# An encoder block in single-precision products: the residual added by accumulating transfers, and the work around the last weights laid out anew

## The chip, the core and the metric

The kernel runs on one core of one Trainium2 chip. The core has a matrix engine (TensorE, "PE" in the profile, with its weight loads as "PEld"), a vector engine (VectorE, "DVE"), an activation engine (ScalarE, "ACT"), a general engine (GpSimd, "POOL") that does no arithmetic here and only issues transfers, and a synchronisation engine (SyncE, "SP") that issues most transfers. 16 DMA engines move the bytes. The metric is device time in microseconds (us) from the first to the last instruction, lower is better; a kernel's time is the median of its runs.

## The reference

One layer of a bidirectional encoder on 512 tokens of width 2048, all in float32:

```python
h = rmsnorm(x, norm_attn)
proj = h @ w_in                                  # q, k, v of two groups of 8 heads
ya = dilated_attention(...); yb = diff_attention(...)
x = x + concat(ya, yb) @ w_out                   # called x1 below
h = rmsnorm(x, norm_ffn)
x = x + (silu(h @ w_gate) * (h @ w_up)) @ w_down # hidden width 5632
return rmsnorm(x, norm_final)
```

The change touches the two last lines alone. `rmsnorm(x, g)` is `x * r * g`, where `r` is one number for each token, the reciprocal root of the mean square. So the gate and up products can be taken of `x1 * g`, without `r`, and `r` can be multiplied in afterwards, token by token.

## The kernel before

**Products.** The matmuls take values of a rounded type (`F32R`). To keep float32's accuracy every operand is split into a high part and the rest: ACT rounds (`hi`), DVE subtracts (`lo = value - hi`), and `mm3` (lines 183 to 186) makes three matmuls of it. A split is therefore one ACT and one DVE instruction for each weight tile, at lines 120 and 121 for weights that go in as they are (`fetch`) and at lines 629 and 630 for weights that are first combined (`make`).

**Stages.** Queries, keys, values and both attentions come first; then the output projection (`unit_out`), which also stores `x1` to memory (`x1_kept`). Then come the gate and up products: 44 units of 128 hidden features each (`unit_gu`). They use a Strassen-like scheme with seven products instead of eight; `make` forms the sums of weights, `keep_combos` those of the activations, which go to memory (`combos`). The down product runs over most hidden features by the same scheme, in five chunks `c` of four or three pairs of feature tiles (`CHUNKS`), each in four units `u` of 512 output columns (`unit_dn`). What is left over goes in without the scheme: two feature tiles ahead of the chunks (`unit_first`) and four behind them (`unit_last`). `unit_last` runs over 4 token tiles `t` and 4 column groups `g`; each of the 16 groups is 12 matmuls of 512 columns, then `to_rest` and `finish`, which adds up the squares for the final norm and, at `g == 3`, scales the token tile and sends it out.

**The running sum.** `unit_first` copies its products to eight tiles `acc[u, l]` (`u` a column group, `l` a half of the tokens); half of each is stored negated, because `add` only adds. Every `unit_dn` adds its products to them. In the last chunk `add_x1` (lines 860 to 867) turns them into the residual sum: two instructions for each of 16 pieces compute `acc * r2 + x1`, with `r2` the token scale for one half and `nr2 = -r2` for the other, and `x1` loaded back by SP. `to_rest` adds the product of `unit_last`, again times `r2`. The scale `r` is thus multiplied in twice: in `unit_gu` into the gate and up values ahead of Silu (line 689, with the tile `rb2` that holds `r` along the tokens), where the up value `c11` and the other up values stay unscaled, and at the end for these.

**Order of the work.** PE's instructions run in the order in which the program lists them. Those of ACT, DVE, SP and POOL are put in order ahead of time by a planner, which simulates the program with a model of costs and takes the earliest listed instruction that is ready by this model; so a transfer or a split can stand well ahead of its place in the program, or behind it. Once planned, each engine runs its list strictly in order, waits included. Splits run three products ahead of PE (`product_of(..., ahead=3)`).

**Places.** Raw weights land in three staging tiles `st` (pool `wst`) or in `m0` to `m5`; split pairs lie in three rotating `hi`/`lo` pairs (`wsh`, `wsl`) and in `m6` to `m9`. The operands of the down product lie in seven large tiles (`cp0` to `cp5` and `w0`). The last eight weight pairs of `order` and the last four activation tiles (`act_tile`) take places that have become free by then: `late_tile` cuts them from `cp` tiles, three places from each; pairs 2, 3 and 4 use `wsh`/`wsl`. All of that is listed by `prepare_last` at one point, product 3 of the last unit (four `act_tile`, the gains of the final norm, two `fetch`), and by the first lines of `unit_last` (the other six `fetch`). Small constants lie in the pool `const`, which is placed first, so its size shifts the tiles behind it.

Of the kernel before, what the change touches and what calls it, by code (L numbers as in the profile page):

```python
# [45 lines left out]
def encoder_block(ctx: ExitStack, tc: tile.TileContext, io):  # L46
# [602 lines left out]
    def unit_gu(f):  # L649
# [23 lines left out]
        def after(i):  # L673
# [13 lines left out]
            elif i == 5:  # L687
                dve.tensor_add(g[:, first], gm[:, first], u2)
                dve.tensor_mul(g, g, pools["rb2"])
                act.activation(g, g, AF.Silu, scale=-1.0)  # L690
                dve.tensor_mul(out[0], c11, g[:, first])
# [48 lines left out]
    nr2 = const.tile([P, NT], F32, name="nr2")  # L740
# [27 lines left out]
    def unit_first():  # L768
# [3 lines left out]
        dve.tensor_scalar_mul(nr2, r2, -1.0)  # L772
        for u in range(DN):
# [11 lines left out]
            for t in range(NT):  # L785
                o = acc[u, t // 2][:, (t % 2) * 512:(t % 2 + 1) * 512]
                act.copy(o[:, :256], b[t][:, :256])
                act.activation(o[:, 256:], b[t][:, 256:], AF.Copy, scale=-1.0)

    def unit_dn(c, u):  # L790
# [17 lines left out]
        def add(h, l, x):  # L808
            dve.tensor_add(r[h, l], flat(x), r[h, l])
# [40 lines left out]
        for i in range(7):  # L850
            product(i, pairs[3:] if apart and i < 4 else pairs)
            after(i)
            if i0 == len(UNITS) - 1 and i == 3:
                prepare_last()
            yield
        if c == len(CHUNKS) - 1:
            for t in range(2):
                add_x1(t, u)

    def add_x1(t, u):  # L860
        x1 = w_tile()
        nc.sync.dma_start(x1, x1_kept[t, u])
        y = rest[t, u] = acc[u, t // 2][:, (t % 2) * 512:(t % 2 + 1) * 512]
        for h, r in enumerate((r2, nr2)):
            s = slice(h * 256, (h + 1) * 256)
            dve.scalar_tensor_tensor(y[:, s], y[:, s], r[:, t:t + 1], x1[:, s], op0=OP.mult, op1=OP.add)

    late = []

    def late_tile():  # L870

        n = len(late)
        if n % 3 == 0:
            late_tile.last = pools["xa"].tile([P, 7, 512], F32R, name=f"cp{(0, 1, 5, 2, 3)[n // 3]}")
        late.append(late_tile.last[:, 2 * (n % 3):2 * (n % 3) + 2].rearrange("p a q -> p (a q)"))
        return late[-1]

    def last_pair(i):
        if 2 <= i < 5:
            return wsh.tile([P, 1024], F32R, name="hi"), wsl.tile([P, 1024], F32R, name="lo")  # L880
        return late_tile(), late_tile()

    def prepare_last():
        for f in range(NF - CF, NF):
            act_tile(f, late_tile())
        load_gfin()
        fetch()
        fetch()
# [184 lines left out]
```

## Time and profile before

| | |
|---|---|
| median of 3 runs | 2227.66 us (2226.16 to 2230.18) |
| the profiled execution, its own time | 2229.82 us |
| its span, first to last instruction | 2228.0 us |
| granted TensorE clock, mean of the span | 0.992 |
| gate and up units | about 866 to 1748 us |
| `unit_first` and the five chunks | about 1748 to 2166.8 us |
| `unit_last` and the end | 2166.8 to 2228.0 us |

A window row of the profile gives a stretch, its length, the busy time of each engine with its number of instructions, then the granted clock (1.00 is full), the DMA engines' busy share and GB/s. A timeline row gives start, duration, engine, line, operation, output and inputs by the program's names, and in brackets the engine's idle time ahead of it and what ended it. A group row gives count, then total busy time and mean duration in ns, then idle time ahead of the group's instructions. Matmul durations overlap, since they are pipelined; the distance of their starts is their cost. Engine names with a "q" are the engine's instruction queue, which issues transfers.

### The profile page before, as it was taken

What the parts mean: (1) busy time and instruction counts of PE and PEld (TensorE: products, weight loads), DVE (VectorE), ACT (ScalarE), POOL (GpSimd) and SP (SyncE); (2) the same over time, 40 slices, a digit from 0 to 9 for tenths busy, and PEclk for the clock granted to TensorE, in tenths of its full rate; (3) what the DMA queues carried; (4) which work ended last, traced back from release to release, by engine and by line L of the source; (5) the groups of instructions that cost most, each with busy time, mean ns of one, the idle gap of its engine ahead of it and who ended that gap; (6) DMA issues with size and microseconds to landing.
All of it is one profiled execution on the core that took longest, in us unless ns stands there. A gap on an engine that the chain in (4) does not pass through costs nothing.

```text
span 2228.0 us, 37887 instructions
## 1 busy us (share of the span) xinstructions
PE 2195.6 (99%) x15754; PEld 2067.2 (93%) x15754; DVE 1663.9 (75%) x2373; ACT 999.4 (45%) x1486; POOL 10.4 (0%) x23
## 2 busy tenths in 40 slices
PE   9999999999999999999999999999999999999997
PEld 8888888888888888999999999999999899999995
DVE  5655555676787447888888888888887597888897
ACT  6333333545555344454444544445444443343443
POOL 0000000000000000000000000000000000000000
PEclk9999999999999999999999999999999999999999
DMA  8222222222222552354454444544445736446344
GB/s 301 84 78 76 85 77 76 76 76 68 67 76 91 165 180 85 124 169 147 132 169 147 165 147 134 170 147 159 151 132 164 312 114 245 156 166 236 114 138 138
DMA packets 86908, 308.59 MB, mean 139 GB/s; under 512 B 10032, under 2 KB 11952, under 8 KB 84304
## 3 DMA queue, kind: packets, MB, share of 16 engines
q1 hardware_dynamic: 81696, 267.11, 36.4%
q0 software_dynamic: 2736, 34.87, 3.8%
q10 hardware_dynamic: 2304, 4.20, 0.5%
q8 instruction: 123, 2.02, 0.4%
q14 instruction: 49, 0.40, 0.1%
HBM read 261.31 MB, written 44.83 MB: 137 GB/s over the span
## 4 chain that ended last, share of the span: by engine, by line
PE 92%; DVE 4%; DMA 2%; ACT 1%; issue 1%; SPq 0%; ACTq 0%; DVEq 0%
PE bank L184 30%; PE bank L186 29%; PE bank L185 29%; PE bank L303 1%; DMA acts_kept<-raw 1%; DVE lo L630 1%; PE bank L403 1%; PE bank L404 1%; DMA st<-w 0%; DVE m L630 0%; PE bank L539 0%; PE bank L428 0%; DMA combos<-y 0%; DMA at<-xT 0%; ACT hi L629 0%
## 5 line engine op out<-in xcount | busy, mean ns | idle before, releaser
L629 ACT CAST hi<-m 128x1024 fp32r<-128x1024 f32 (+1 forms) x208 | 215.0, 1038 | 252.9 <-PE bank L185 125.0
L184 PE MATMUL bank<-cp,hi 128*128 128x256 f32 x1116 | 314.1, 281 | 0.0
L185 PE MATMUL bank<-cp,hi 128*128 128x256 f32 x1116 | 312.2, 280 | 0.0
L186 PE MATMUL bank<-cp,lo 128*128 128x256 f32 x1116 | 312.2, 280 | 0.0
L630 DVE TENSOR_TENSOR lo<-m,hi 128x1024 fp32r<-128x1024 f32 (+1 forms) x208 | 249.6, 1201 | 61.8 <-ACT hi L629 61.5
L121 DVE TENSOR_TENSOR lo<-st,hi 128x1024 fp32r<-128x1024 f32 (+1 forms) x136 | 165.1, 1214 | 141.0 <-ACT hi L120 140.2
L120 ACT CAST hi<-st 128x1024 fp32r<-128x1024 f32 (+1 forms) x136 | 141.7, 1042 | 192.8 <-PE bank L185 74.8
L185 PE MATMUL bank<-lo,cp 128*128 128x256 f32 (+1 forms) x738 | 211.4, 286 | 4.2 <-DVE lo L630 2.7
L184 PE MATMUL bank<-hi,cp 128*128 128x256 f32 (+1 forms) x738 | 211.3, 286 | 0.3 <-ACT hi L120 0.3
L184 PEld LDWEIGHTS bank<-cp,hi 128*128 128x128 f32 x1116 | 211.1, 189 | 0.3 <-DVE wk L679 0.2
L186 PE MATMUL bank<-hi,cp 128*128 128x256 f32 (+1 forms) x738 | 211.0, 286 | 0.0
L185 PEld LDWEIGHTS bank<-cp,hi 128*128 128x128 f32 x1116 | 210.6, 189 | 0.0
L186 PEld LDWEIGHTS bank<-cp,lo 128*128 128x128 f32 x1116 | 210.5, 189 | 0.0
L184 PE MATMUL bank<-xt,hi 128*128 128x512 f32 x512 | 206.3, 403 | 0.0
L184 PE MATMUL bank<-cp,m 128*128 128x256 f32 x732 | 205.6, 281 | 0.1
L186 PE MATMUL bank<-cp,m 128*128 128x256 f32 x732 | 204.2, 279 | 0.0
L185 PE MATMUL bank<-cp,m 128*128 128x256 f32 x732 | 204.2, 279 | 0.0
L186 PE MATMUL bank<-xt,lo 128*128 128x512 f32 x512 | 200.4, 391 | 0.0
L185 PE MATMUL bank<-xt,hi 128*128 128x512 f32 x512 | 199.9, 391 | 0.0
L629 ACT CAST m<-m 128x1024 fp32r<-128x1024 f32 (+1 forms) x112 | 116.8, 1043 | 148.6 <-PE bank L185 88.6
L630 DVE TENSOR_TENSOR m<-m,m 128x1024 fp32r<-128x1024 f32 (+1 forms) x112 | 135.3, 1208 | 41.4 <-ACT m L629 41.2
L185 PE MATMUL bank<-lo,xt 128*128 128x256 f32 x512 | 145.1, 283 | 0.6 <-DVE lo L121 0.6
(276 smaller groups left out, 5920.7 us busy)
## 6 DMA issues: line engine op xcount, KB each, us to landing
st<-w SPq DMA_DIRECT2D x199, 512.0 KB, 3.7
m<-w SPq DMA_DIRECT2D x180, 512.0 KB, 4.4
cp<-combos POOLq DMA_DIRECT2D x17, 1792.0 KB, 16.6
combos<-y SPq DMA_DIRECT2D x57, 512.0 KB, 4.4
combos<-y SPq DMA_DIRECT2D x19, 256.0 KB, 5.2
m<-w SPq DMA_DIRECT2D x12, 384.0 KB, 3.2
at<-x SPq DMA_DIRECT2D x8, 512.0 KB, 9.0
wk<-x SPq DMA_DIRECT2D x16, 256.0 KB, 5.3
```

What stands on the lines that cost most here:

```text
L120: act.copy(hi[:, s], st[:, s])
L121: dve.tensor_sub(lo[:, s], st[:, s], hi[:, s].bitcast(F32))
L184: pe.matmul(out, lh, rh, start=start, stop=False, **kw)
L185: pe.matmul(out, lh, rl, start=False, stop=False, **kw)
L186: pe.matmul(out, ll, rh, start=False, stop=stop, **kw)
L303: pe.transpose(b[:, j * P:(j + 1) * P], prob[:, j * P:(j + 1) * P], ident)
L403: pe.matmul(b, q[:, qs], kh[:, cs], start=True, stop=False)
L404: pe.matmul(b, q[:, qs], kl[:, cs], start=False, stop=True)
L629: act.copy(hi[:, :n], w[name])
L630: dve.tensor_sub(lo[:, :n], w[name], hi[:, :n].bitcast(F32))
```

## The change

1. `unit_gu` multiplies `g` with `rb2` once more after Silu, so that the products carry the token scale of the up value too.
2. `unit_first` copies 512 columns in one piece with their sign; `add` subtracts where it used to add to a negated sum. `nr2` is gone.
3. `add_x1` is two POOL transfers for each column group. They read `x1_kept` and add to `acc` in place. They are listed in chunk 2: unit `u` adds to the sum of column group `(u + 2) % 4`. The 16 SP loads and the 32 DVE instructions of before are gone, and `to_rest` is a plain addition.
4. The last weights and activations are listed at set points from chunk 3 on, and take other places: pair 0 `m7` and `m9`, pairs 1 and 2 and the activations thirds of `cp0`, `cp1` and `cp5`, pair 3 and half of pair 4 the raw-weight places `m0` to `m5`, pairs 5, 6 and 7 `wsh`/`wsl`. Three `fetch` stay at the head of `unit_last`.
5. `finish` writes the product with the gains to another tile than the one that ScalarE squares, and the odd output pieces are sent by ACT's queue.
6. A spare tile `gap` of 8 floats is put into `const`.

```diff
@@ unit_gu
                 dve.tensor_mul(g, g, pools["rb2"])
                 act.activation(g, g, AF.Silu, scale=-1.0)
+                dve.tensor_mul(g, g, pools["rb2"])
                 dve.tensor_mul(out[0], c11, g[:, first])
...
-    nr2 = const.tile([P, NT], F32, name="nr2")
...
-        dve.tensor_scalar_mul(nr2, r2, -1.0)
...
-                o = acc[u, t // 2][:, (t % 2) * 512:(t % 2 + 1) * 512]
-                act.copy(o[:, :256], b[t][:, :256])
-                act.activation(o[:, 256:], b[t][:, 256:], AF.Copy, scale=-1.0)
+                act.copy(acc[u, t // 2][:, (t % 2) * 512:(t % 2 + 1) * 512], b[t])
@@ unit_dn
         def add(h, l, x):
-            dve.tensor_add(r[h, l], flat(x), r[h, l])
+            if h == 1:
+                dve.tensor_add(r[h, l], r[h, l], flat(x))
+            else:
+                dve.tensor_sub(r[h, l], r[h, l], flat(x))
...
             after(i)
-            if i0 == len(UNITS) - 1 and i == 3:
-                prepare_last()
+            if c == 2 and i == 1:
+                add_x1((u + 2) % DN)
+            prepare_last(c, u, i)
             yield
-        if c == len(CHUNKS) - 1:
-            for t in range(2):
-                add_x1(t, u)
-
-    def add_x1(t, u):
-        x1 = w_tile()
-        nc.sync.dma_start(x1, x1_kept[t, u])
-        y = rest[t, u] = acc[u, t // 2][:, (t % 2) * 512:(t % 2 + 1) * 512]
-        for h, r in enumerate((r2, nr2)):
-            s = slice(h * 256, (h + 1) * 256)
-            dve.scalar_tensor_tensor(y[:, s], y[:, s], r[:, t:t + 1], x1[:, s], op0=OP.mult, op1=OP.add)
...
+    def add_x1(u):
+        for l in range(2):
+            pool.dma_start(acc[u, l].rearrange("p (t q) -> p t q", t=2),
+                           x1_kept[2 * l:2 * l + 2, u].rearrange("t p q -> p t q"), accum_op=OP.add)
+
+    free, left, spare, gains = [], [0, 1, 5], [], []
 
     def last_pair(i):
-        if 2 <= i < 5:
-            return wsh.tile([P, 1024], F32R, name="hi"), wsl.tile([P, 1024], F32R, name="lo")
-        return late_tile(), late_tile()
-
-    def prepare_last():
-        for f in range(NF - CF, NF):
-            act_tile(f, late_tile())
-        load_gfin()
-        fetch()
-        fetch()
+        if i == 0:
+            return place(7, F32R), place(9, F32R)
+        if i < 3:
+            return take(), take()
+        if i == 3:
+            return place(at[0] % 6, F32R), place((at[0] + 1) % 6, F32R)
+        if i == 4:
+            return take(), place((at[0] + 2) % 6, F32R)
+        return wsh.tile([P, 1024], F32R, name="hi"), wsl.tile([P, 1024], F32R, name="lo")
+
+    def take():
+        if not free:
+            w = pools["xa"].tile([P, 7, 512], F32R, name=f"cp{left.pop(0)}")
+            free.extend(w[:, 2 * j:2 * j + 2].rearrange("p a q -> p (a q)") for j in range(3))
+        return free.pop(0)
+
+    def prepare_last(c, u, i):
+        if (c, u, i) in ((3, 3, 3), (4, 1, 1), (4, 1, 4), (4, 3, 3), (4, 3, 4)):
+            fetch()
+        if (c, u, i) == (4, 2, 4):
+            load_gfin()
+        if c == 4 and u == 0 and i in (1, 4):
+            for f in range(2):
+                act_tile(NF - CF + f + (i == 4) * 2, take())
 
     def to_rest(t, g, b):
-        dve.scalar_tensor_tensor(rest[t, g], b, r2[:, t:t + 1], rest[t, g], op0=OP.mult, op1=OP.add)
+        y = rest[t, g] = acc[g, t // 2][:, (t % 2) * 512:(t % 2 + 1) * 512]
+        dve.tensor_add(y, b, y)
...
-                if t < 2:
-                    add_x1(2 + t, g)
                 to_rest(t, g, b)
                 finish(t, g)
...
@@ finish
         act.activation(jk, y, AF.Square, accum_out=col)
-        dve.tensor_mul(y, y, gfin[g // 2][:, (g % 2) * 512:(g % 2 + 1) * 512])
+        z = done_y[t, g] = rest[t - 1, g] if t else spare[g] if g < 3 else w_tile()
+        dve.tensor_mul(z, y, gfin[g // 2][:, (g % 2) * 512:(g % 2 + 1) * 512])
...
             for c in range(4):
+                z = done_y[t, c]
+                o = io["out"][t * P:(t + 1) * P, c * 512:(c + 1) * 512]
                 if c % 2:
-                    act.activation(rest[t, c], rest[t, c], AF.Copy, scale=r)
+                    act.activation(z, z, AF.Copy, scale=r)
+                    act.dma_start(o, z)
                 else:
-                    dve.tensor_scalar_mul(rest[t, c], rest[t, c], r)
-                nc.sync.dma_start(io["out"][t * P:(t + 1) * P, c * 512:(c + 1) * 512], rest[t, c])
+                    dve.tensor_scalar_mul(z, z, r)
+                    nc.sync.dma_start(o, z)
...
     gsub = const.tile([P, 1], F32, name="gsub")
+    dve.memset(const.tile([P, 8], F32, name="gap"), 0.0)
```

More of the change, by code (lines that the diff above doesn't have):

```diff
@@ L868, in encoder_block @@
[L868 to L876, printed above, removed]
-    def last_pair(i):
-        if 2 <= i < 5:
-            return wsh.tile([P, 1024], F32R, name="hi"), wsl.tile([P, 1024], F32R, name="lo")
-        return late_tile(), late_tile()
-    def prepare_last():
-        for f in range(NF - CF, NF):
-            act_tile(f, late_tile())
-        load_gfin()
-        fetch()
-        fetch()
+    def add_x1(u):
+        for l in range(2):
+            pool.dma_start(acc[u, l].rearrange("p (t q) -> p t q", t=2),
+                           x1_kept[2 * l:2 * l + 2, u].rearrange("t p q -> p t q"), accum_op=OP.add)
@@ L911, in load_gfin @@
     def load_gfin():
-        gains = pools["mx"].tile([P, 7, 512], F32, name="w0")
+        gains.append(pools["mx"].tile([P, 7, 512], F32, name="w0"))
+        spare.extend(gains[0][:, j] for j in range(4, 7))
         for j in range(2):
-            t = gains[:, 2 * j:2 * j + 2].rearrange("p a q -> p (a q)")
+            t = gains[0][:, 2 * j:2 * j + 2].rearrange("p a q -> p (a q)")
             nc.sync.dma_start(t, io["gfin"][:, j * 1024:(j + 1) * 1024].to_broadcast([P, 1024]))
@@ L918, in encoder_block @@
     ssq3 = const.tile([P, 16], F32, name="ssq3")
-    so_far = {}
+    so_far, done_y = {}, {}
     def finish(t, g):
```

## The prediction

> **What bounds the kernel now.** I read the page first: the busy line and the chain of waits.
>
> ```profile
> PE 2195.6 (99%) x15754; PEld 2067.2 (93%) x15754; DVE 1663.9 (75%) x2373; ACT 999.4 (45%) x1486; POOL 10.4 (0%) x23
> ...
> PE 92%; DVE 4%; DMA 2%; ACT 1%; issue 1%; SPq 0%; ACTq 0%; DVEq 0%
> ```
>
> PE sets the time. The change removes no matmul, so it can win only where PE waits, where PE runs slowly, and behind the last matmul. The windows by stage tell where that is.
>
> ```profile
> 880.00:1390.00 510.00, 510.00 (x4286) 509.93 (x4286) 431.67 (x520) 245.31 (x327) 0.00 (x0) 1.00 0.45 146
> ...
> 2105.00:2166.80 61.80, 61.80 (x527) 61.80 (x526) 60.95 (x88) 28.32 (x39) 0.00 (x0) 1.00 0.44 144
> 2166.80:2180.00 13.20, 10.15 (x38) 6.22 (x36) 11.58 (x17) 7.26 (x10) 0.00 (x0) 1.00 0.74 238
> 2180.00:2190.00 10.00, 8.94 (x37) 6.76 (x37) 9.06 (x21) 3.18 (x8) 0.00 (x0) 1.00 0.35 114
> 2190.00:2217.60 27.60, 27.60 (x121) 22.33 (x120) 22.37 (x68) 11.04 (x26) 0.00 (x0) 1.00 0.41 134
> 2217.60:2228.00 10.40, 0.17 (x1) 0.00 (x0) 4.12 (x16) 2.06 (x4) 0.00 (x0) 0.71 0.29 101
> ```
>
> The gate and up stage has no idle PE. The last stage has: from 2166.8 to 2190, 75 matmuls fall in 23.2 us, against 121 in the next 27.6. The timeline of PE shows the stage's first matmul, its waits, two undisturbed stretches, and its last matmul.
>
> ```profile
> 2166.83 0.39 PE L184 MATMUL bank<-cp,cp 128*128 128x512 f32 x1
> ...
> 2171.97 0.51 PE L185 MATMUL bank<-lo,cp 128*128 128x512 f32 x1 [0.76 <-DVE lo L121]
> ...
> 2178.60 0.50 PE L185 MATMUL bank<-cp,cp 128*128 128x512 f32 x1 [0.78 <-DVE cp L121]
> 2181.39 0.51 PE L185 MATMUL bank<-cp,cp 128*128 128x512 f32 x1 [0.76 <-DVE cp L121]
> ...
> 2194.66 0.39 PE L186 MATMUL bank<-cp,cp 128*128 128x512 f32 x1
> ...
> 2196.70 0.39 PE L186 MATMUL bank<-cp,cp 128*128 128x512 f32 x1
> ...
> 2199.22 0.39 PE L185 MATMUL bank<-lo,cp 128*128 128x512 f32 x1
> ...
> 2199.92 0.39 PE L185 MATMUL bank<-lo,cp 128*128 128x512 f32 x1
> ...
> 2217.38 0.39 PE L186 MATMUL bank<-cp,cp 128*128 128x512 f32 x1
> ```
>
> Undisturbed matmuls start 2.04/9 = 0.2267 us apart with weights in `cp` tiles, 0.70/3 = 0.2333 with weights in `hi`/`lo`. Line 121 is the split of a fetched weight, so PE waits for the last weights.
>
> **The last stage, fed in time.** It has 16 x 12 = 192 matmuls, 24 for each of the eight weight pairs. Three pairs lie in `hi`/`lo` before: 120 x 0.2267 + 72 x 0.2333 = 44.0 us undisturbed. It takes 2217.61 - 2166.83 = 50.8, so 6.8 are lost. Why are the splits late? Here they, the 32 instructions of line 866 (`add_x1`) and the ordinary work share DVE:
>
> ```profile
> 2166.80:2228.00 61.20, 8.44 (x19) 0.95 0.45 147
> sum 123.00, DVE 14.24; mean DVE 7.12
> ...
> L121 DVE TENSOR_TENSOR cp<-st,cp 128x1024 fp32r<-128x1024 f32 x4 | 4.9, 1222 | 1.4 <-ACT cp L120 1.4
> ```
>
> That is the windows view for line 866 alone (19 of its 32 fall behind 2166.8), and a DVE group of the last stage. The splits also wait for ACT, and ACT for weights through three staging tiles. Afterwards line 866 is gone and five of eight pairs are listed before the stage. The other three are first needed 30, 36 and 42 matmuls into it, at 6.8, 8.2 and 9.5 us, and each takes 1.2 us of DVE. So I cost these waits at nothing: -6.8. New places take some back: pairs 0, 3, 5, 6, 7 and a third of 4 no longer have weights in `cp`. I know no price for `m` places beside activations in `cp`; it lies between 0.2267 and 0.2333. I take 0.2333, since in the list above only `cp` with `cp` has the shorter distance: 128 against 72 such matmuls, 56 x 0.0066 = +0.4. Term: **-6.4** (-6.8 to -6.3 by that bound, nearer 0 if splits stay late).
>
> **The end.** Behind the last matmul stand the last sum, the square, the product with the gains, the root and four outputs.
>
> ```profile
> 2218.67 0.63 ACT L926 ACTIVATE wk<-w 128x512 f32<-128x512 f32 x1 [1.55 <-DVE w L891]
> 2219.42 0.69 DVE L927 TENSOR_TENSOR w<-w,w 128x512 f32<-128x512 f32 x1 [0.85 <-ACT wk L926]
> 2220.03 0.15 DVE L929 SCALAR_TENSOR_TENSOR sm<-ssq,sm 128x1 f32<-128x1 f32 x1
> ...
> 2222.51 0.33 SPq L938 DMA_DIRECT2D out<-y  x1
> ...
> 2223.41 0.89 SPq L938 DMA_DIRECT2D out<-w  x2
> ```
>
> The product at line 927 overwrites what ACT squares, so it starts behind the square. With its own output it runs under the square, and line 929 starts 2220.03 - 2219.42 = 0.6 us sooner. Four issues on SP take 2224.30 - 2222.51 = 1.8 us. On two queues the last can go about 0.5 us sooner (ACT's second scaling and issue stand behind its first issue); bounds 0 and 0.9. Term: **-1.1** (-0.6 to -1.5). The Trainium skill ("DMA: Bandwidth & Descriptors", section "Issuing engines are not separate DMA queues") says that a second issuing queue saves only the time of issuing, as all transfers share the same engines. By the rule alone it saves at most the 0.9 of two issues, and nothing where the engines are the limit, so that the gain would be 0.5 smaller and the time 2220.9; no run here has shown output on two queues.
>
> **Gate and up: one more product, 44 times.** Its twin at line 689:
>
> ```profile
> L689 DVE TENSOR_TENSOR wk<-wk,rb 128x512 f32<-128x512 f32 x44 | 30.1, 684 | 0.1
> ```
>
> It is 30.1 us of DVE in all. In the window from 880, 510 us hold some 25.6 units; DVE goes from 432 to 449 busy of 510. That hides it: **0**. Queued behind it are the products at lines 691 and 696 and the next splits, which run three matmul products ahead; without that cover the price would be 0.6 us a unit, 26 us. Hence the upper bound is that of a filled DVE, which 449 of 510 excludes. Activations of the last unit go to memory up to 0.6 us later.
>
> **`unit_first`.** ACT's copies into `raw` wait for that very transfer; then PE waits.
>
> ```profile
> 1768.41 0.37 ACT L787 COPY raw<-bank 128x256 f32<-128x256 f32 x1 [6.82 <-DMA acts_kept<-raw]
> 1768.68 0.39 ACT L788 ACTIVATE raw<-bank 128x256 f32<-128x256 f32 x1
> ...
> 1778.49 0.58 PE L185 MATMUL bank<-lo,cp 128*128 128x256 f32 x1 [2.75 <-DVE lo L630]
> ...
> 2139.47 0.59 ACT L825 COPY wk<-bank 128x512 f32<-128x512 f32 x1 [0.87 <-PE bank L186]
> 2139.96 0.83 ACT L629 CAST hi<-st 128x768 fp32r<-128x768 f32 x1
> ```
>
> Sixteen half copies, 0.27 us from start to start, become eight whole ones at 0.49 (the 128x512 copy of line 825): 4.3 - 3.9 = 0.4 less. Against it stands the transfer's 0 to 0.6. I take **-0.3** (-0.4 to +0.2). Subtracting in place of adding is the same form of instruction: 0. The spare tile's memset stands among the constants at the start: 0.
>
> **Chunk 4's vector work.** DVE is busy 60.95 of 61.8 us there, so this is where fetches can hurt. Gone are 13 of line 866 (14.24 - 8.44 = 5.8 us). Before, one of line 121 fell in this stretch; now four are listed there (and one in chunk 3): 3 x 1.2 = +3.7. The four activation splits were there already. On balance DVE has 2 us less; but staging tiles and ACT are now shared with units that still load. I allow **+0.5** (0 to +3).
>
> **The accumulating transfers.** None stands in the trace. The nearest rows are the loads issued by POOL and the loads that they replace, a window at the first chunk boundary, where the same loads run, the raw weights that SP loads at the second, a split made of these, and the copy that ACT makes of the unit's first product:
>
> ```profile
> 1937.06 0.53 POOL L766 DMA_DIRECT2D cp<-combos  x1 [82.42 <-PE bank L186]
> ...
> cp<-combos POOLq DMA_DIRECT2D x17, 1792.0 KB, 16.6
> wk<-x_kept SPq DMA_DIRECT2D x16, 256.0 KB, 3.7
> ...
> 1867.70:1873.70 6.00, 5.99 (x28) 6.00 (x29) 4.42 (x6) 0.49 (x1) 0.00 (x0) 0.50 0.98 412
> ...
> 1952.22 16.83 SPq L600 DMA_DIRECT2D m<-w  x3
> ...
> 1965.17 2.35 DVE L630 TENSOR_TENSOR lo<-m,hi 128x1024 fp32r<-128x1024 f32 x2
> ...
> 1967.26 0.59 ACT L825 COPY wk<-bank 128x512 f32<-128x512 f32 x1 [1.72 <-PE bank L186]
> ```
>
> The first two of eight go through POOL's queue near the four loads of the chunk boundary; behind POOL's wait for PE stand only these loads. A sum is needed again by `add` two units later, some 40 us. At the 412 GB/s of the full engines two of 512 KB take 2.5 us. Between that and several times that I take the plain end, as the bytes are the same: **0** (0 to +12, rival 3).
>
> **Sum.** -6.4 - 1.1 - 0.3 + 0.5 = -7.3 against the profiled execution's own 2229.82 (its span of 2228.0 and 1.8 around it): 2222.5. That execution lies 2.2 above the median of the runs shown, 2227.66; the same step from there gives **2220.4**.
>
> **The rivals.** A change of 0.2% is 4.5 us, about what a measurement of this kernel can tell from none.
>
> *1. The last stage stays half starved* (the set points do not do what they say): the planner may still place splits late. Half of 6.8 comes back: 2223.8. For it: staging stays three tiles. Against: 19 of line 866 leave the stage.
>
> *2. Faster still: a boundary's wait goes.* PE waits three times at chunk boundaries, and the clock halves afterwards.
>
> ```profile
> PE bank L184 <- DVE wk L829: 8.5, 3, 2.8
> ```
>
> Waits of 0.8 us cost no clock in the last stage (1.00 in its rows above); after one of 2.8, just before the window from 1867.7 above, PE ran 6 us at half (0.50). Should the planner's new order shorten one such wait, its 2.8 and about 3 of clock go too: 2220.4 - 5 = 2215. The order there is not touched by the change, so this is unlikely. The Trainium skill ("TensorE: Matmul & The Clock Gate", section "Why this matters for your kernels") warns of idle gaps above about 3 us; the trace agrees with its 2.8.
>
> *3. Slower: the accumulating transfers hold up weights.* Place: the boundary of chunk 2. Three raw-weight loads issue from 1952 while the POOL loads fill the engines. If accumulating takes six times as long as a plain load, 1 MB holds the queues 15 us instead of 2.5. The first of the two splits shown above ends at 1966.35 (one is 1.2 us). Its product is the third of its unit; the copy on ACT at 1967.26 marks the end of the first, and the second has 24 matmuls, 2.8 us, so it is used at about 1969.9: a lead of 3.5 us. So PE waits 12.5 - 3.5 = 9 and then loses 3 of clock: +12, 2232. It decides from a factor of 2.4 (2.5 us times 1.4 is the lead); it outweighs the gain from four. For it: the engines are full at such a boundary (share 0.98). Against: the planner may issue the first ones before the boundary.
>
> *4. Slower: places shift.* The two distances of 0.2267 and 0.2333 show that places cost. If the spare tile did not replace `nr2` exactly, 10,600 matmuls of 256 columns at half of these 6.6 ns more give +35: 2255. Both tiles take one 32-byte step of the layout, so tiles behind `const` stay.
>
> **How the numbers follow.** Forecast 55%, rival 1 20%, rival 2 8%, rival 3 7%, rival 4 3%, and 7% that chunk 4 makes new long waits (+7, no gain left: 2227). Range 2216.5 to 2226: the forecast's bounds, rival 1 and part of rival 2. Faster by over 0.2%: nearly all of the forecast, rival 2 and under half of rival 1, 0.71. Within 0.2%: the rest of rival 1 and chunk 4's waits, 0.19. Slower: rivals 3 and 4, 0.10.
>
> **What would show it.** Line 121 no longer ahead of PE's waits in the last stage, and 44 to 45 us from its first to its last matmul; line 929 right behind the last square; no new wait of PE in chunks 2 to 4; the distance between matmuls of the gate stage as before. Wrong would be: waits on staged loads in chunk 4, a wait for `acc` in chunk 2 or 3, a longer matmul distance.

## The result and the profile after

The changed kernel is slower. Its median is 2232.62 us (2228.82 to 2236.53) against 2226.16 us (2220.37 to 2232.30) for the kernel before in the same runs: a ratio of 1.0032 with a 95% interval of 1.0019 to 1.0046, or some 7 us more. The forecast was 2220.4 us and faster. The profiled execution of the kernel after took 2233.29 us with a span of 2231.5.

The page of the kernel after, busy line and chain of waits:

```profile
PE 2193.1 (98%) x15754; PEld 2061.7 (92%) x15754; DVE 1679.8 (75%) x2385; ACT 999.2 (45%) x1470; POOL 20.2 (1%) x31
...
PE 15%; DVE 3%; DMA 2%; issue 1%; ACT 0%; ACTq 0%; DVEq 0%
```

The busy line says little: PE works as long as before, and DVE's share is still 75%. The chain was followed back over only a fifth of the span here, so it can't be set beside that of the kernel before. The windows by stage of the kernel after answer those shown of before (the same columns):

```profile
880.00:1390.00 510.00, 506.92 (x4238) 504.45 (x4239) 441.92 (x537) 244.03 (x325) 0.00 (x0) 1.00 0.44 147
...
2105.00:2177.40 72.40, 68.19 (x576) 66.74 (x575) 67.66 (x87) 34.33 (x45) 0.00 (x0) 1.00 0.42 130
2177.40:2190.00 12.60, 12.60 (x57) 10.24 (x56) 8.23 (x14) 3.81 (x9) 0.00 (x0) 1.00 0.00 0
2190.00:2221.60 31.60, 31.60 (x139) 25.62 (x137) 23.05 (x68) 12.13 (x30) 0.00 (x0) 1.00 0.30 101
2221.60:2231.50 9.90, 0.38 (x2) 0.00 (x0) 3.93 (x14) 2.06 (x4) 0.00 (x0) 0.71 0.31 106
```

The last stage is full now: its two rows have no idle PE. But the gate and up stage, which had none before (510.00 of 510), has 3.1 us of it in this window, and the stretch of chunk 4 has 4.2 (72.40 - 68.19). What PE waits for there, and in chunk 2, is in the waits of the kernel after, asked for three stretches (waiting for, us in all, times, longest): first the gate stage, then chunk 4, then chunk 2 behind its boundary.

```profile
PE bank L184 <- DVE wk L686: 4.6, 12, 0.7
...
PE bank L184 <- DVE sums L809: 1.7, 1, 1.7
PE bank L185 <- DVE lo L630: 1.0, 2, 0.5
PE bank L184 <- ACT wk L825: 0.9, 1, 0.9
PE bank L185 <- DVE m L630: 0.6, 1, 0.6
...
PE bank L184 <- DVE sums L809: 1.0, 1, 1.0
PE bank L185 <- DVE lo L630: 0.9, 1, 0.9
```

In the same stretches of the kernel before there is none of these waits. The three waits of 2.8 us at the chunk boundaries are in both.

For the lengths of the stages, take the starts of ACT's first copy of a unit (line 675 in gate and up, line 825 in the down product), of the first and last 512-column matmul behind them, and the end of the span. They give this table, in us, for all kernels of this document, each from one profiled execution. Some of what differs is chance. Each of chunks 0 to 3 holds none, 3.4 or 6.8 us of half clock (0.50 in the windows view), and the 256-column matmuls of chunks 0 and 2 start either 113.3 or 117.8 ns apart (117.3 to 120.0 in e7_no_spacer); both differ where the instructions are the same. The first unit of gate and up holds 3.4 us of half clock, but 6.8 in before, e2_before_scale, e9_one_queue and e12_boundary. Chunk 4 and the last stage hold none. Five kernels with the same gate stage (after, e4, e6, e8, e9) spread from 861.8 to 864.4 us.

| | gate and up | chunks 0 to 3 | chunk 4 | last stage | end | ratio to before, 95% interval |
|---|---|---|---|---|---|---|
| before | 855.6 | 335.3 | 57.0 | 50.6 | 10.7 | 1 |
| after | 863.1 | 332.2 | 61.9 | 44.2 | 9.9 | 1.0032 (1.0019 to 1.0046) |
| e1_no_scale | 854.6 | 331.2 | 61.5 | 44.2 | 9.9 | 0.9994 (0.9982 to 1.0005) |
| e2_before_scale | 864.0 | 335.2 | 57.0 | 50.5 | 10.6 | 1.0028 (1.0017 to 1.0039) |
| e3_own_piece | 853.7 | 331.4 | 61.1 | 44.2 | 9.9 | 0.9995 (0.9985 to 1.0005) |
| e4_late_points | 861.8 | 333.6 | 57.4 | 45.4 | 10.0 | 1.0014 (1.0004 to 1.0024) |
| e5_both | 853.7 | 331.4 | 57.5 | 45.2 | 10.0 | 0.9980 (0.9970 to 0.9990) |
| e6_no_accum | 862.4 | 327.5 | 60.9 | 44.2 | 10.0 | 1.0018 (1.0006 to 1.0030) |
| e7_no_spacer | 866.8 | 334.3 | 61.4 | 44.4 | 10.0 | 1.0072 (1.0058 to 1.0086) |
| e8_own_staging | 861.8 | 333.0 | 58.6 | 44.2 | 10.0 | 1.0014 (1.0003 to 1.0026) |
| e9_one_queue | 864.4 | 334.3 | 62.4 | 44.2 | 10.0 | one execution only |
| e10_swap | 853.7 | 335.3 | 58.8 | 45.3 | 10.0 | 0.9990 (0.9981 to 0.9999) |
| e11_moved | 853.8 | 329.5 | 57.4 | 45.2 | 10.0 | 0.9983 (0.9974 to 0.9992) |
| e12_boundary | 855.0 | 328.0 | 57.5 | 45.0 | 9.9 | 0.9968 (0.9956 to 0.9979) |

So the change won 6.4 us in the last stage and 0.8 at the end, where 6.4 and 1.1 were forecast, and lost 7.5 us in gate and up and 4.9 in chunk 4, which were forecast at 0 and 0.5. By luck of the clock the 7.5 is too small: the first gate unit took 18.1 us before, with 6.8 us of half clock, and 16.9 after, with 3.4. The other 42 units took 837.5 us before and 846.2 after, which is 8.8 more.

### The profile page after: what moved, and what is told of

Read it like the earlier page. It is cut to its first block, busy times and chain, and to the rows that moved or that the text cites. A ratio compares the mean times of both kernels' runs of the same rounds, so it can differ in the third digit from the quotient of the medians.

```text
span 2231.5 us, 37922 instructions
## 1 busy us (share of the span) xinstructions
PE 2193.1 (98%) x15754; PEld 2061.7 (92%) x15754; DVE 1679.8 (75%) x2385; ACT 999.2 (45%) x1470; POOL 20.2 (1%) x31
## 5 line engine op out<-in xcount | busy, mean ns | idle before, releaser
L184 PE MATMUL bank<-cp,hi 128*128 128x256 f32 x1116 | 314.9, 282 | 2.6 <-DVE wk L686 2.4
L184 PEld LDWEIGHTS bank<-cp,hi 128*128 128x128 f32 x1116 | 210.7, 189 | 5.2 <-DVE wk L686 4.9
L184 PE MATMUL bank<-hi,cp 128*128 128x256 f32 (+1 forms) x738 | 209.8, 284 | 3.5 <-DVE sums L809 2.7
L184 PE MATMUL bank<-cp,m 128*128 128x256 f32 x732 | 206.0, 281 | 2.5 <-DVE wk L686 2.2
L184 PE MATMUL bank<-xt,hi 128*128 128x512 f32 x512 | 206.3, 403 | 0.0
L184 PEld LDWEIGHTS bank<-hi,cp 128*128 128x128 f32 x738 | 141.1, 191 | 5.3 <-issue 3.0
```

Of the source, the lines that this page charges most:

```text
L184: pe.matmul(out, lh, rh, start=start, stop=False, **kw)
```

## The experiments

### Gate and up: the one extra product

How can a product of 0.68 us delay PE when DVE has 60 us to spare in such a window? Look at one pair of units. The kernel before, timelines of ACT, DVE and SP, in the order of what depends on what:

```profile
1109.28 0.63 ACT L690 ACTIVATE wk<-wk 128x512 f32<-128x512 f32 x1 [1.49 <-DVE wk L689]
...
1110.63 0.41 DVE L696 TENSOR_TENSOR raw<-bank,wk 128x256 f32<-128x256 f32 x1
...
1113.41 3.07 SPq L735 DMA_DIRECT2D combos<-y  x3
...
1118.79 0.62 ACT L643 CAST y<-sums 128x512 fp32r<-128x512 f32 x1 [2.18 <-DMA combos<-y]
...
1119.44 0.69 DVE L644 TENSOR_TENSOR y<-sums,y 128x512 fp32r<-128x512 f32 x1 [1.84 <-ACT y L643]
...
1125.53 0.42 DVE L686 TENSOR_TENSOR wk<-bank,wk 128x256 f32<-128x256 f32 x1
```

And the same chain in the kernel after, with the new product at line 691 and the matmul that waits:

```profile
1112.17 0.63 ACT L690 ACTIVATE wk<-wk 128x512 f32<-128x512 f32 x1 [1.54 <-DVE wk L689]
...
1113.19 0.68 DVE L691 TENSOR_TENSOR wk<-wk,rb 128x512 f32<-128x512 f32 x1
1113.80 1.22 DVE L630 TENSOR_TENSOR lo<-st,hi 128x1024 fp32r<-128x1024 f32 x1
1114.93 0.42 DVE L692 TENSOR_TENSOR raw<-wk 128x256 f32<-128x256 f32 x1
1115.27 0.41 DVE L697 TENSOR_TENSOR raw<-bank,wk 128x256 f32<-128x256 f32 x1
...
1118.55 2.09 SPq L736 DMA_DIRECT2D combos<-y  x3
...
1124.15 0.62 ACT L643 CAST y<-sums 128x512 fp32r<-128x512 f32 x1 [1.87 <-DMA combos<-y]
...
1124.81 0.69 DVE L644 TENSOR_TENSOR y<-sums,y 128x512 fp32r<-128x512 f32 x1 [1.53 <-ACT y L643]
...
1129.28 0.42 DVE L686 TENSOR_TENSOR wk<-bank,wk 128x256 f32<-128x256 f32 x1
...
1129.75 0.38 PE L184 MATMUL bank<-cp,m 128*128 128x256 f32 x1 [0.20 <-DVE wk L686]
```

Behind every second unit `keep_combos` makes four pieces, but there are only three `y` tiles. The fourth piece waits until the store of the first has landed (ACT line 643, idle before it for DMA `combos<-y`), and DVE, in order, waits for that piece (line 644). Everything listed behind it, line 686 among it, is late by as much; and PE needs line 686, which reads the bank that the last product of the unit goes on with. From Silu to the last up product it took 1110.63 - 1109.28 = 1.35 us before and takes 1115.27 - 1112.17 = 3.10 after: the product itself, and a split of 1.2 us that the planner now puts between it and its user. DVE's idle time lies inside the chain, while it waits for the store, and is no reserve. The list of waits counts only gaps behind the modelled end of a matmul, 4.6 us in 12 of them; by the first copies nearly every pair of units is longer, 40.3 us on average against 39.9 before.

**e1_no_scale** takes the product away:

```diff
                 act.activation(g, g, AF.Silu, scale=-1.0)
-                dve.tensor_mul(g, g, pools["rb2"])
```

> The kernel after, without the second product with rb2 in unit_gu; the token scale of the up value is left out, everything else stays. In the profiles a pair of gate and up units takes 40.2 us after and 39.86 us before. Theory A (the product sits in DVE's queue ahead of the last up product and of keep_combos, so the first combos store goes later, the fourth piece of keep_combos waits for that store's tile, and the bank-freeing sum at line 686 comes late for PE): a pair is back at 39.86 us, the gate stage 7.5 us shorter, the whole kernel about 2225. Rival B (the stage lost its 7.5 us to something else that the change moved, such as places of tiles or the clock): a pair stays at 40.2 us and the time at 2232. Both expect the same for the later chunks: chunk 4 as in the kernel after, within 1 us.

**e2_before_scale** adds it, and nothing else, to the kernel before:

```diff
                 act.activation(g, g, AF.Silu, scale=-1.0)
+                dve.tensor_mul(g, g, pools["rb2"])
```

> The kernel before, with the second product with rb2 in unit_gu alone added (the up value's token scale is then applied twice). Theory A: the product alone does the damage, a pair of units goes from 39.86 to about 40.2 us, the gate stage is 7.5 us longer, the whole kernel about 2234 against 2227 (ratio 1.003). Rival B: a pair stays at 39.86 us and the ratio at 1.000.

Both came out as theory A says. Without the product the gate stage takes 854.6 us and the ratio is 0.9994; with it in the kernel before the stage takes 864.0 and the ratio is 1.0028. Chunk 4 stayed as in the respective kernel. So the product does it, alone. That doesn't yet tell whether DVE is too full or the chain too long.

**e3_own_piece** keeps the product and shortens the chain. One of the four pieces fills half of a `y` tile; it gets a tile of its own, 2 KB in each partition, in space that was free:

```diff
+        pools["yh"] = stage("yh", 1, "right")
...
-            y = y_tile(F32R).rearrange("p (n q) -> p n q", n=2)[:, :n]
+            if n == 1:
+                y = pools["yh"].tile([P, 1, 512], F32R, name="yh")
+            else:
+                y = y_tile(F32R).rearrange("p (n q) -> p n q", n=2)
```

> The kernel after, with a tile of its own for the one combos piece that fills only half of a y tile, so the three y tiles serve the three other pieces and no piece waits for a store of its own pair; the second product stays, no other tile moves. Theory A: ACT's waits at line 643 for a combos store (36.5 us in all, 19 times) go, the new PE waits for line 686 go, a pair is back at 39.86 us, the time about 2225. Rival C (DVE has simply too much work in a unit of 19.93 us, or the planner lists its work in a worse order): ACT's waits go, but a pair stays at 40.1 to 40.2 us and the time at 2231 to 2233.

The gate stage takes 853.7 us and the ratio is 0.9995. ACT no longer waits for a store there, and no wait for line 686 is left. The window of e3_own_piece for the gate stage:

```profile
880.00:1390.00 510.00, 510.00 (x4290) 509.76 (x4289) 449.34 (x544) 245.48 (x328) 0.00 (x0) 1.00 0.43 146
```

DVE does 449.34 us of work in 510, just what the prediction had worked out, and PE idles nowhere. Rival C falls: DVE was never too full. The one tile more is worth 9.4 us of the stage to the kernel after.

### Chunk 4: the set points

**e4_late_points** lists the last splits where the kernel before does:

```diff
-        if (c, u, i) in ((3, 3, 3), (4, 1, 1), (4, 1, 4), (4, 3, 3), (4, 3, 4)):
-            fetch()
-        if (c, u, i) == (4, 2, 4):
-            load_gfin()
-        if c == 4 and u == 0 and i in (1, 4):
-            for f in range(2):
-                act_tile(NF - CF + f + (i == 4) * 2, take())
+        if (c, u, i) == (4, 3, 3):
+            for f in range(NF - CF, NF):
+                act_tile(f, take())
+            load_gfin()
+            fetch()
+            fetch()
```

> The kernel after, with the last splits listed where the kernel before lists them (four activations, the gains and two weights at product 3 of the last unit, six weights at the head of the last stage); places and everything else as after. Theory S (in chunk 4 the listed loads hold the three staging tiles, so the units' own raw weights land late): units (4,1) and (4,2) go from 17.1 and 18.2 back to 14.84 us, chunk 4 is 5.7 us shorter; the last stage loses what the fetches wait for, 2 to 6 us, since line 866 no longer competes on DVE: the sum is 2229 to 2233. Rival T (chunk 4 lost its time to something else, such as the changed sums or late accumulating transfers): the units stay at 17 and 18 us, the last stage is longer, the time 2234 to 2239.

Chunk 4 is back at 57.4 us, its units at 14.84. The last stage takes 45.4, only 1.2 more than with the set points and 5.2 less than before. So theory S holds, and its guess for the last stage was still too high. Where the time went shows in the transfers and in what ACT waits for, in the kernel after (SP's queue, then ACT, then PE):

```profile
2117.82 1.96 SPq L745 DMA_DIRECT2D st<-acts_kept  x2
...
2127.02 0.33 SPq L600 DMA_DIRECT2D st<-w  x1
2130.18 4.85 SPq L119 DMA_DIRECT2D st<-w  x2
...
2127.93 0.84 ACT L629 CAST m<-st 128x768 fp32r<-128x768 f32 x1 [4.37 <-DVE st L610]
...
2143.03 0.36 PE L184 MATMUL bank<-hi,cp 128*128 128x256 f32 x1 [1.71 <-DVE sums L809]
```

The raw weight that unit (4,1) needs through a staging tile is sent for at 2127.02, 11.5 us behind the first copy of chunk 4 (2115.48). The four activation tiles had the staging tiles. In e4_late_points the same transfer goes 2.3 us behind that copy (2112.87):

```profile
2115.21 0.33 SPq L600 DMA_DIRECT2D st<-w  x1
```

**e8_own_staging** leaves the points and gives the activations a staging tile of their own:

```diff
-            src = wst.tile([P, 1024], F32, name="st")[:, :512]
+            src = pools["yh"].tile([P, 512], F32, name="yh")
```

> The kernel after, with the activation tiles loaded through a staging tile of their own (512 columns) in place of the three st tiles; the set points stay. Theory S1 (the four activation loads take the st tiles from the units' raw weights): most of the 5.7 us of chunk 4 comes back, units (4,1) and (4,2) at 15 to 16 us, ratio to before 1.001. Rival S2 (the listed fetches of 1024 columns, two in unit (4,1), are what holds the st tiles): units (4,1) and (4,2) stay within 0.7 us of 17.1 and 18.2 us, ratio 1.003.

Chunk 4 takes 58.6 us, so 3.3 of the 4.5 us that e4_late_points won come back: mostly S1. Whether the rest lies at the listed fetches, which still take `st` tiles, or at the activations' single tile was not separated. Chunk 4 and the last stage together take 102.8 us in both kernels, so the set points are as good as the late list once the activations have their own tile. Its single units can't be read as I had expected, because the copies themselves moved (16.6, 14.3 and 16.8 us); the sum of the chunk can.

**e5_both** is e3_own_piece and e4_late_points in one.

> The kernel after with the two edits of e3_own_piece and e4_late_points together. If the two losses are separate (theories A and S): a pair of gate units at 39.86 us, units of chunk 4 at 14.84 us, the last stage at 45.4 us, and the gains add: ratio to before 1.0032 - 0.0037 - 0.0018 = 0.9977, about 2220 to 2222 us. If they overlap (one delay was hidden behind the other): ratio 0.9990 to 1.0000.

The ratio is 0.9980, against 0.9977 worked out: the two losses are separate, and they add (the interval only touches the other case, at 0.9990). With 2220.0 us median against 2224.54 for the kernel before in the same runs, and by its ratio, this version beats both kernels.

### The accumulating transfers

**e6_no_accum** leaves them out:

```diff
-            if c == 2 and i == 1:
-                add_x1((u + 2) % DN)
```

> The kernel after without the eight accumulating transfers; the residual is left out. My theory: they cost PE nothing (0 to 1 us), chunks 2 and 3 stay at 84.1 and 78.1 us within the change of clock, the ratio to before at 1.003. Rival 3 of the prediction (they hold up raw weights): the small waits for lines 630 and 809 in chunks 2 and 3, about 2 us, go and the time falls by 2 to 5 us.

I had expected nothing, and rival 3 of the prediction is nearer. Both waits of chunk 2 are gone, and the chunk takes 81.3 us in place of 84.1, with one stretch of half clock of 3.4 us in each. The ratio of 1.0018 fits, though its interval overlaps that of the kernel after. In the kernel after (POOL, DVE and PE, then the landing times of what was sent between 1950 and 1951.8 and between 1956 and 1961: KB each, median us to landing):

```profile
1950.44 1.21 POOL L860 DMA_DIRECT2D w<-x_kept  x1 [5.21 <-issue]
...
1971.62 1.23 DVE L610 TENSOR_TENSOR st<-m,st 128x1024 f32<-128x1024 f32 x1 [4.27 <-DMA m<-w]
...
1974.64 0.39 PE L185 MATMUL bank<-lo,cp 128*128 128x256 f32 x1 [0.87 <-DVE lo L630]
1987.05 0.36 PE L184 MATMUL bank<-hi,cp 128*128 128x256 f32 x1 [0.96 <-DVE sums L809]
...
w<-x_kept POOLq DMA_DIRECT2D x1, 512.0 KB, 21.2
...
m<-w SPq DMA_DIRECT2D x2, 512.0 KB, 11.5
```

One accumulating transfer goes out right behind the four operand loads of chunk 2 and lands after 21.2 us. Not all of that is its own: the operand loads issued ahead of it by POOL land one after another, the last at 1966.4, and it lands 5.2 us behind that. The raw weights sent beside it take 11.5 us; in e6_no_accum the two that answer to them take 9.4. This is no chance of one execution: in the eight traces with that transfer there they take 10.9 to 11.7 us each, and in before, e2_before_scale, e6_no_accum and e11_moved 8.7 to 10.0.

**e11_moved** is e5_both with these transfers listed behind product 6 of units (2,1) to (2,3) and product 1 of (3,1):

```diff
-            if c == 2 and i == 1:
-                add_x1((u + 2) % DN)
+            if (c, u, i) in X1_POINTS:   # {(2,1,6): 0, (2,2,6): 1, (2,3,6): 2, (3,1,1): 3}
+                add_x1(X1_POINTS[c, u, i])
```

> e5_both with the accumulating transfers listed elsewhere: behind product 6 of units (2,1), (2,2) and (2,3) and behind product 1 of (3,1), so that none is in flight while chunk 2's operands and first raw weights load. The kernel without them lost two waits of PE in chunk 2 (0.87 and 0.96 us by the row, 1.0 and 1.3 us between matmul starts). Theory X (their cost is that one transfer shares the DMA engines with the loads of the boundary): both waits go, chunk 2 falls from 85.6 to about 83 us, the time by 2 to 3 us to about 2217.5. Rival Y (accumulating transfers cost wherever they stand): the waits come later, in chunk 2 or 3, and the time stays within 1 us of e5_both.

Chunk 2 falls from 85.6 to 81.3 us, chunk 3 rises from 77.0 to 78.6, where a wait of 0.9 us has come up. That is X for the most part, with a share of Y. But only 2.1 of the 4.2 us in chunk 2 are the two waits (0.7 and 1.4 us in e5_both). Behind the second of them the matmuls of e5_both start 117.8 ns apart to the end of the chunk, and 113.3 ns ahead of it; in e11_moved they stay at 113.3. The same 20 us in e5_both, then in e11_moved:

```profile
1980.00:2000.00 20.00, 20.00 (x172) 20.00 (x171) 17.79 (x19) 8.32 (x9) 2.38 (x2) 1.00 0.64 160
...
1980.00:2000.00 20.00, 20.00 (x179) 20.00 (x178) 17.52 (x19) 8.65 (x10) 2.39 (x2) 1.00 0.64 163
```

That is worth another 1.7 us. Why a wait can leave the slower distance behind was not found out; in the kernel after it came with one of the two waits and went with the other. The median is 2218.9 against 2220.0, but the two ratios (0.9983 and 0.9980) can't be told apart.

### The boundaries

Rival 2 of the prediction said that a boundary's wait might go, with the clock that it costs. The change didn't do that; can it be done?

**e10_swap** is e5_both with product 22 between s2 and s1 in the first unit of chunks 1 to 4:

```diff
+    SWAPPED = PRODUCTS[:4] + ("22", "s1", "s4")
```

> e5_both, and in the first unit of chunks 1 to 4 the product 22 is made and multiplied ahead of s1, so that its 24 matmuls (2.8 us) lie between s2 and s1 and cover the sum u2, for which PE waits 2.8 us at three boundaries (8.5 us in all). Theory W (the wait is only the sum's lateness, and the half clock that follows each of these waits comes from them): the three waits shrink to under 0.8 us each, the half-clock stretches behind them go, and the time falls by 8.5 us and 10 to 20 us of clock, to about 2195 to 2203. Rival V (the waits go but the half-clock stretches come at set times anyway): 6 to 9 us less, about 2213. Rival U (the sum that frees the bank of 22 is as late as u2, or the splits come late in the new order): under 3 us.

It came out as rival U. The waits for `u2` are gone, but the sum that frees the bank of 22 is late in its place (`PE bank L184 <- DVE y L819`, 8.8 us in five waits), and the ratio is 0.9990, no better than e5_both. Its trace also has the slower distance of 117.8 ns in most of chunks 0 and 2. The reason stands in the timeline of e5_both at such a boundary (DVE, then PE):

```profile
1943.53 1.22 DVE L631 TENSOR_TENSOR m<-st,m 128x1024 fp32r<-128x1024 f32 x1
1944.66 1.22 DVE L631 TENSOR_TENSOR lo<-m,hi 128x1024 fp32r<-128x1024 f32 x1
1945.80 0.68 DVE L833 TENSOR_TENSOR wk<-bank,wk 128x512 f32<-128x512 f32 x1
...
1946.63 0.36 PE L184 MATMUL bank<-m,cp 128*128 128x256 f32 x1 [2.85 <-DVE wk L833]
```

DVE does two splits ahead of the sum that PE waits for, and PE can't use the second of them for 2.8 us yet. It is a matter of order on DVE.

**e12_boundary** is e11_moved with another order there:

```diff
-            wh, wl = product_of(i0, i, 3 - i if some is early else 3)
+            wh, wl = product_of(i0, i, 3 - i if some is early or apart and i < 3 else 3)
...
-        for i in range(7):
+        for i in (0, 2, 1, 3, 4, 5, 6) if apart else range(7):
```

and the sums of `after(2)` and `after(3)` other than `u2` wait until `after(4)`. `apart` holds for the first unit of chunk 4 too, so the edit reaches one chunk more than its expectation says; chunk 4 takes 57.5 us as ahead of it.

> e11_moved, and in the first unit of chunks 1 to 3 the sum u2, for which PE waits 2.8 us, is put ahead of the splits in DVE's order: the fourth pair of s2 is multiplied ahead of that of s3, the splits of the next products are listed behind u2, and four sums wait until s1 is multiplied. By the timeline of e5_both u2 could then be done at 1943.0 in place of 1946.5 and PE would wait for the split of s1 instead, until about 1944.8. Theory W (each wait shrinks to about 1.2 us, and so short a wait brings no half clock): 3 x 1.7 = 5 us of waits and 3 us of clock behind each go, the time falls by 10 to 14 us, to about 2205. Rival V (the half clock comes all the same): 4 to 6 us less. Rival U (another sum or split is late in place of u2): under 3 us less.

The three boundary waits are 1.28 us each in place of 2.84, and the clock behind each of them is full, in chunk 3 up to the next long wait. In e12_boundary, PE's waits at the boundary of chunk 2 and behind that of chunk 3, and the window behind the former; then the window of e5_both behind its wait of 2.85 us:

```profile
1945.70 0.39 PE L185 MATMUL bank<-m,cp 128*128 128x256 f32 x1 [1.28 <-DVE m L631]
...
2043.60 0.39 PE L185 MATMUL bank<-lo,cp 128*128 128x256 f32 x1 [2.77 <-DVE lo L631]
...
1946.00:1960.00 14.00, 13.64 (x121) 13.45 (x120) 11.98 (x15) 5.31 (x7) 1.22 (x1) 1.00 0.91 319
```

```profile
1946.70:1950.10 3.40, 3.40 (x22) 3.40 (x23) 3.40 (x5) 0.00 (x0) 0.00 (x0) 0.69 0.99 417
```

The mechanism is that of theory W, but the gain isn't: sums and splits pushed back are late 14 to 27 us further on, above all the wait of 2.77 us in chunk 3, which is followed by a half clock of its own. The waits of chunks 1 to 3 add up to 9.2 us, against 10.1 in e11_moved, so by its size this is rival U. The median is 2216.27 us, 2.6 less than e11_moved, with a ratio to before of 0.9968 (0.9956 to 0.9979); the two intervals overlap a little. It has the lowest ratio of all these kernels, 0.6% below the kernel after.

### The spacer and the second queue

**e7_no_spacer** takes the spare tile away:

```diff
-    dve.memset(const.tile([P, 8], F32, name="gap"), 0.0)
```

> The kernel after without the spare tile gap, so every tile on the left side behind the constants lies 32 bytes lower; nothing else changes. Theory P (places set the distance of matmuls): the distance of the 256-column matmuls with split weights grows from 118.6 ns, by up to 1.5 ns, which is 0 to 16 us on 10,600 matmuls, and a pair of gate units is above 40.2 us. Rival Q (32 bytes make no difference): distances, stages and time as in the kernel after, ratio to before 1.003.

Theory P holds. The mean distance of undisturbed matmuls in the gate stage is 119.7 ns against 118.5 in the kernel after and 118.6 before, worked out from their starts. The window of e7_no_spacer shows it too:

```profile
880.00:1390.00 510.00, 509.72 (x4235) 507.98 (x4234) 442.00 (x537) 242.95 (x324) 0.00 (x0) 1.00 0.43 146
```

PE hardly idles, and yet 4235 matmuls take what 4290 take in e3_own_piece. 1.2 ns on the stage's 7392 matmuls is 8.9 us; the stage grew by 3.7, and the slower PE waits less for line 686 (twice, 1.4 us, in place of 12 times, 4.6 us). The ratio of 1.0072 is 0.4% above that of the kernel after, some 9 us; the two profiled executions differ by 4.1, so part of it was not located.

**e9_one_queue** sends all output by SP:

```diff
-                    act.dma_start(o, z)
-                else:
-                    dve.tensor_scalar_mul(z, z, r)
-                    nc.sync.dma_start(o, z)
+                else:
+                    dve.tensor_scalar_mul(z, z, r)
+                nc.sync.dma_start(o, z)
```

> The kernel after, with all output pieces sent by SP. My prediction's step: from the last matmul's start to the end of the span it takes 0.5 us more than the 9.91 us of the kernel after, about 10.4. Rival (a second queue saves nothing, since the transfers are the limit): 9.9 us. No other stage changes.

The end takes 10.0 us, within what the kernels with two queues show (9.9 to 10.0). In the kernel after, then in e9_one_queue: the first scaling of the last token tile and the last issue.

```profile
2225.47 0.72 ACT L940 ACTIVATE sums<-sums,sm 128x512 f32<-128x512 f32 x1 [2.01 <-DVE sm L172]
...
2226.83 0.34 ACTq L941 DMA_DIRECT2D out<-w  x1
```

```profile
2227.34 0.72 ACT L940 ACTIVATE sums<-sums,sm 128x512 f32<-128x512 f32 x1 [2.01 <-DVE sm L172]
...
2228.75 0.90 SPq L943 DMA_DIRECT2D out<-w  x2
```

With two queues the last issue ends 1.7 us behind the first scaling, with one 2.3, but the span ends 6.0 us behind it in both (2231.49 - 2225.47 and 2233.39 - 2227.34). The issue came sooner and the end did not. The rule of the Trainium skill that the prediction named ("DMA: Bandwidth & Descriptors", section "Issuing engines are not separate DMA queues") says that a second issuer saves only issue time; the trace agrees, and here even that was worth nothing.

## Why the prediction was wrong

**The last stage, -6.4:** right in size (50.55 to 44.19 us), and no wait is left in it. The reasons were in part wrong. The prediction named two together, line 866 leaving DVE and five pairs listed ahead of the stage; e4_late_points has 5.2 us of the gain without the second, and the set points bring 1.2. Nor is it shown that DVE's share of line 866 did the rest, for in the trace of before DVE takes up a split as soon as ACT has rounded, and ACT waits for the raw weight:

```profile
2169.61 1.05 ACT L120 CAST hi<-st 128x1024 fp32r<-128x1024 f32 x1 [1.95 <-DMA st<-w]
...
2170.69 1.22 DVE L121 TENSOR_TENSOR lo<-st,hi 128x1024 fp32r<-128x1024 f32 x1
```

PE's wait at 2171.97 is for this split. The loads came late: SP sent the first of the eight 6.2 us ahead of the stage before, with loads of `x1` among them in its queue, and 11.1 us ahead in e4_late_points (2159.15 against 2170.28). Line 866, its 16 loads and the places all changed together there, and no run separates them.

**The end, -1.1:** -0.8 measured. The product under the square works as described: both start at 2222.74 in the kernel after, and the last sum of squares starts 1.9 us behind the last matmul's start (2223.49 - 2221.58), against 2.65 before (2220.03 - 2217.38). The 0.5 for the second queue wasn't there.

**Gate and up, 0:** this step failed, and it turned the sign: +7.5 us, or 8.8 without the unit in which the clock differed. It said that a DVE busy for 449 of 510 us hides a product of 0.6 us, and it excluded the upper end of the range by that share. The share was right to the microsecond, and PE waited all the same. What the step left out is who waits for whom. It listed what is queued behind the new instruction (the up products, the splits) and stopped at the splits' lead; it didn't follow the queue to the next instruction that frees a bank for PE, line 686, nor see that DVE already waited in front of it for a store (the rows of ACT and DVE above were in the trace of before). The price was not the instruction's 0.6 us in all 44 units either, but what was left of some 1.75 us behind every second unit when the chain's slack was used up.

**`unit_first`, -0.3:** the time from the last gate unit's copy to the first of chunk 0 is 43.0 us in the kernel before and 41.3 to 42.6 in the others that have the change. A gain of 0.3 to 1.7; but e2_before_scale, which has the old copies, takes 42.6 too, so the copies' part is not shown.

**Chunk 4, +0.5 (0 to +3):** +4.9 us. The step counted DVE's work on balance, as 2 us less. In fact it stayed about the same, since six splits of line 121 fall in the chunk and not four (6.8 us in place of 1.2, against the 6.2 us of line 866 that are gone). That was not the cost, as DVE is busy for 58.6 of 61.9 us where it was for 56.3 of 57.0. The step named the staging tiles without costing them. A staging tile is held from the issue of its load to the end of its split, and the listed loads took it ahead of a raw weight that PE needed sooner. That is the case of "new long waits" that the prediction gave 7%.

**The accumulating transfers, 0:** some 2.5 us in chunk 2 of the kernel after, and up to 4.2 where the slower distance stayed (e5_both against e11_moved). Rival 3 had the place and the mechanism. Its size was wrong: no 9 us, but two waits just under 1 us, and that its 2232 us is nearly the measured median is luck. As to its factor of six, the last transfer of the boundary lands 18.4 us behind the chunk's first copy, against 15.4 in e6_no_accum; 512 KB at 412 GB/s are 1.3 us, so the factor is about 2.4, an estimate from these numbers. I had the weights 3.5 us ahead of need. The one that DVE waited for came 2.8 us later (11.7 against 8.9) and PE waited 0.9, so the lead was nearer 2 us.

**Subtraction and spacer, 0:** line 809 takes 0.68 to 0.69 us as the addition of before and as the subtraction of after, and the spacer is what keeps the places at 0. Rival 4 was right that places cost and too high in size: 1.2 ns for each gate matmul, where it took 3.3.

The measured terms are -6.4 - 0.8 + 7.5 + 4.9 + 2.5 and about -1 for `unit_first`: +6.7, against 6.5 between the medians. So close a match is luck: the terms come from single executions, and the two profiled ones differ by 3.4 us in their spans, with other stretches of half clock and other distances in chunks 0 to 3.

## What to carry to other kernels

Idle time of an engine is no reserve until one knows where it lies. Before an instruction is added to an in-order engine, look for the next instruction behind it that frees something for the engine that sets the time, and for any wait that already stands between the two; here the cure was one more small buffer and not less work. Early loads through a shared staging pool are not free either: ask which load they go ahead of.

## What the runs showed of the hardware

- The distance of matmuls depends on where their operands lie: 32 bytes lower for every tile on one side changed it from 118.5 to 119.7 ns at 256 columns, in all units of the gate stage. No run showed why.
- With the places unchanged, the 256-column matmuls of chunks 0 and 2 still start 113.3 or 117.8 ns apart, and keep to one of the two between waits. In chunk 0 the kernel after had 113.3 and e9_one_queue 117.8, with the same instructions up to there; in chunk 2 of e5_both it changed at a wait of 1.4 us, in chunk 0 of e8_own_staging at one of 0.35. At some 670 matmuls a chunk that is 3 us. No run showed why.
- A wait of 1.28 us was followed by no half clock at the three boundaries of e12_boundary. Of the 36 boundary waits of 2.8 us in the twelve kernels that keep them, 29 were followed by 3.4 or 6.8 us of it and seven by none, among them that of chunk 1 in e5_both. The length alone doesn't decide: at the start of chunk 0 waits of 1.9 us were followed by 3.4 us of it in the kernel after and e5_both, and one of 3.2 us by none in e10_swap. The Trainium skill ("TensorE: Matmul & The Clock Gate", section "Why this matters for your kernels") warns of gaps above about 3 us; here 2.8 was enough in most cases.
- Accumulating transfers of 512 KB took 5.7 to 9.9 us to land by the medians of their four groups in the kernel after; raw weights of 512 KB took 3.7 to 4.5. So they are slower, by something under a factor of three with other traffic beside them; at what rate alone was not measured.
